# A reciprocal RMS spread by two fp32r products instead of fp32 ones, and four reorderings, in a hybrid S5 / RG-LRU decoder layer

## The chip, the core and the metric

One NeuronCore of a Trainium2 chip runs the whole layer. Its engines work side by side: TensorE (PE in the profile; PEld is its weight loading), VectorE (DVE), ScalarE (ACT), GpSimd (POOL) and SyncE (SP, which issues most DMAs). Each engine takes its instructions in the order in which the program wrote them; engines wait for each other by semaphores. The metric is device time in microseconds (us) of one execution, and the times given are medians over executions.

## What is computed

One layer, batch 1, 1024 tokens, model width 1024, all in float32:

```python
h = rms_norm(x, g_pre)
s5_x, s5_g, lru_x, lru_g, gate_s, gate_l = split(h @ w_in)      # w_in: 1024 x 5632
y_s = s5_ssm(s5_x, ...)                                         # 32 groups, 64 complex states each
glu_a, glu_b = split(gelu(y_s) @ w_glu)
z_s = (glu_a * sigmoid(glu_b) * silu(s5_g)) @ w_bs
y_l = rg_lru(causal_depthwise_conv(lru_x, conv_w, conv_b), ...) # 1280 channels
z_l = (y_l * silu(lru_g)) @ w_bl
merged = sigmoid(gate_s) * z_s + sigmoid(gate_l) * z_l
x = x + rms_norm(merged @ w_out, g_post)
x = x + (p @ w_ple) * sigmoid(x @ w_ple_gate)
```

`rms_norm(x, g)` is x * rsqrt(mean(x*x) + 1e-6) * g for each token.

## The kernel before

**Layout and products.** Everything is kept transposed: channels on the 128 partitions, tokens along the free axis in two halves of 512 (`HALF`). A matrix product of float32 quality is made of three products in the format fp32r (`three`, L314): each operand is split into a high part, rounded to fp32r, and a low part, the remainder; high x high, high x low and low x high are summed in PSUM. ScalarE makes a high part by a copy (L222, L311, L728, L1364), VectorE the low part by a subtraction (L234, L312, L733, L1371).

**Weights.** `weight_plan` (L37) lists all weight blocks as quads of four 128x128 blocks, in the order of use. `Weights` loads them in raw chunks through SP's queue (four raw buffers), splits them into a ring of six quads, and keeps some quads ahead of TensorE (`ahead`, L244). For w_bs, w_out and the first half of w_ple_gate (`BY_DMA`) the low part is not made by VectorE: ScalarE writes the negated weights into the low part's place after the high copy (L225), and a GpSimd DMA adds the raw weights onto it (L226). Some products for w_bl and w_out use sums of weight blocks, made by GpSimd (`sum`, L179, `add` at L194, marked by the quad "O2"): a quad's sums are issued only when all quads ahead of it have been split (L186).

**Order.** TensorE, VectorE, ScalarE and GpSimd run in the order written out by hand (`manual_schedule`, L480). Work beside the main products is put into generators, which `tick` (L328) advances by one step at each group of products.

**The start.** Eight fp32 warm-up products (L496), then p @ w_ple, column by column (m = 0..7, L755): each column is a PSUM tile `ps_ple` of two banks from a pool of three (`wide`). p comes in four quarters, two blocks of channels k by two halves of tokens; the order of loads is at L504, the first quarter on ScalarE's DMA queue, the rest on SP's. A dictionary `plan` (L747) says what follows each column: squares of x (`square`, L702) and their additions on VectorE (L713), splits of further weight quads (`weights`), and evictions of finished columns (`evict`, L741, by ScalarE to SBUF and by DMA to `ple_d`).

**The reciprocal RMS and its spread.** `tok_rstd` (L383) is a generator of three steps, used once ahead of the input projections ("pre", all 1024 tokens, eight chunks) and once for each token half of the output norm ("post1", then "post0", four chunks each). Step 1: products of the summed squares with a column of ones (`pst`, L388) put the sums of 128 tokens on the 128 partitions. Step 2: variance, square root on ScalarE (L393), reciprocal and one Newton step on VectorE (L394 to L398) give r; then, for each chunk, the identity matrix times r, a diagonal matrix (L401, VectorE). Step 3: an all-ones fp32 matrix times each diagonal matrix (L406) puts r of each token onto all 128 partitions, in the PSUM tile `psb`, one 128x128 product for each chunk. For "pre", steps 1 and 2 are issued after column 5 of w_ple and step 3 inside column 7. Then `h_hi` (L724) scales x by r (VectorE, L727) and splits it, and the first columns of w_in (`ps_u`) begin.

**The end.** merged @ w_out runs as a sequence of `product` calls (L1492) with operands T1 to T4, B11 to B22. `post_half(1)` (L1544) scales the second token half's mix by r and adds x, row by row (L1562, L1563), splitting each row for the last product. `gate_half(1)` (L1569) computes sigmoid(x @ w_ple_gate) for that half, `post_half(0)` advances meanwhile, then `gate_half(0)` follows. In `gate_half(1)` the first two output columns are computed side by side (L1575): the first four rows k of column 0, the same of column 1, then the last four of each. `finish` (L1588) applies the sigmoid on ScalarE, multiplies by p @ w_ple and adds x on VectorE. ScalarE's functions live in tables; changing between square root and sigmoid costs an ACT_TABLE_LOAD.

Of the kernel before, what the change touches and what calls it, by code (L numbers as in the profile page):

```python
# [17 lines left out]
P = 128  # L18
# [18 lines left out]
def weight_plan():  # L37
# [70 lines left out]
    for h in range(2):  # L108
        if not h:
            for ks in (lo, hi):  # L110
                cut(chunk(col("w_ple_gate", 0, ks) + col("w_ple_gate", 1, ks)))
        for c in cs[0 if h else 2:]:
            cut(c)
# [18 lines left out]

LAST = chunk_users()


class Weights:
# [42 lines left out]
    def sum(self, upto):  # L179
        G = self.nc.gpsimd  # L180
        while len(self.ready) <= min(upto, len(QUADS) - 1):
# [3 lines left out]
            s = self.sums  # L185
            if q[0] == "O2" and len(self.done) < i:  # L186
                return
# [25 lines left out]
    def make(self, upto):  # L213
        nc = self.nc
        while len(self.done) <= min(upto, len(QUADS) - 1):
            i = len(self.done)
            self.sum(i)
            src, n = self.ready[i]
            t = self.ring.tile([P, 2, 4, P], F32R, tag="q", name=f"wq{i}")
            hi = t[:, 0].rearrange("p b m -> p (b m)")[:, :n * P]  # L220
            lo = t[:, 1].rearrange("p b m -> p (b m)")[:, :n * P]
            nc.scalar.activation(hi, src, AF.Copy)  # L222
            q = QUADS[i]
            if q[0] == "plain" and BLOCKS[q[1][0]][0] in self.BY_DMA and i < len(QUADS) - 2 * ND:
                nc.scalar.activation(lo, src, AF.Copy, scale=-1.0)  # L225
                nc.gpsimd.dma_start(lo.bitcast(F32), src, accum_op=ALU.add)  # L226
            else:
                self.owed.append((i, lo, src, hi))
            self.done.append(t)
# [23 lines left out]
def tile_hybrid_trunk(  # L253
# [22 lines left out]
    def page(i, name, dt=F32R):  # L276
        return page_pool[i].tile([P, 2 * NT], dt, tag=f"pg{i}", name=name)
# [16 lines left out]
    ones = cst([P, P], "ones", 1.0)  # L294
    ident = cst([P, P], "ident")
    make_identity(nc, ident)
    halfpi = cst([P, 1], "halfpi", math.pi / 2)
    cp_t = cst([P, sum(n for _, n in CPAR)], "cp_t")
    sp8 = cst([P, NL], "sp8")
    nsp8 = cst([P, NL], "nsp8")  # L300
    cp = {}
    o = 0
# [80 lines left out]
    def tok_rstd(v, ssqs, n, name, res, diag):  # L383
# [5 lines left out]
        yield  # L389
        v = v.rearrange("p (i n) -> p i n", i=4)  # L390
        var, r, t, sd = (v[:, i, :nch] for i in range(4))
# [6 lines left out]
        V.tensor_tensor(r, r, t, ALU.mult)  # L398
        diag = diag.rearrange("p (c t) -> p c t", c=nch)
        for c in range(nch):  # L400
            V.tensor_scalar(diag[:, c, :], ident, r[:, c:c + 1], None, ALU.mult)  # L401
        yield
        for h in range(n // HT):
            pb = px.tile([P, HT], F32, tag="px", name=f"psb_{name}_{h}")
            for c in range(4):
                T.matmul(pb[:, c * P:(c + 1) * P], ones, diag[:, 4 * h + c, :], start=True, stop=True)  # L406
            res.append(pb)
# [68 lines left out]
    pt = scratch[:, :NPT]  # L476
    braw = page(7, "braw", F32)

# [16 lines left out]
    warm = px.tile([P, HT], F32, tag="px", name="warm")  # L495
    for _ in range(8):  # L496
        T.matmul(warm[:, :P], ones, ones, start=True, stop=True)
# [5 lines left out]
    W.fetch(0)  # L503
    for k in range(2):  # L504
        for h in range(2):
            (nc.sync if k or h else nc.scalar).dma_start(pf[:, k, HALF[h]], p[k * P:(k + 1) * P, HALF[h]])
    load_x(range(0, 3))
# [17 lines left out]
    V.tensor_tensor(p_lo[:, 0, HALF[0]], pf[:, 0, HALF[0]], p_hi[:, 0, HALF[0]].bitcast(F32), ALU.subtract)  # L525
    for k in range(2):
        for h in range(0 if k else 1, 2):
            split(p_hi[:, k, HALF[h]], p_lo[:, k, HALF[h]], pf[:, k, HALF[h]])
# [187 lines left out]
    ssqs = [ssq]  # L716
    stats = tok_rstd(pro.tile([P, 4 * ND], F32, name="rs_pre"), ssqs, NT, "pre", rb, sdp[:, 1])
    hq = {}
# [36 lines left out]
    for m in range(ND):  # L755
        if m % 2 == 0:
            wb = W.next()
        ps = wide(f"ps_ple{m}")
        rows_ps.append(ps)
        for k in range(2):  # L760
            for h in range(2):
                three(ps[:, HALF[h]], wb[2 * (m % 2) + k], (p_hi[:, k, HALF[h]], p_lo[:, k, HALF[h]]), k == 0, k == 1,
                      xl_last=m == 0)
            if k == 0 and m == 7:
                next(stats)
        if m == 5:
            next(stats)
            next(stats)
        for f, a in plan[m]:
            f(a)  # L770
            if f is square:
                add_squares(1)
        if m == 3:
            add_squares(0)
        W.fetch(9)
# [4 lines left out]
    evict(7)  # L780
    h_hi(1)
    nc.sync.dma_start(braw[:, :1024], spar[:, NPT:NPT + 1024])
    S.activation(d_skip, pt[:16, NPT - 32:], AF.Copy)
# [760 lines left out]
    def post_half(h):  # L1544
# [4 lines left out]
        add_square(h)  # L1549
        st = tok_rstd(dg[:, 2, 32 * h:32 * h + 32], [ssq[h]], HT, f"post{h}", out_, dg[:, h, :])  # L1550
        if h == 0:
# [17 lines left out]
    def gate_half(h, hl):  # L1569
# [4 lines left out]
        if h:  # L1574
            for n in range(4):  # L1575
                q, m = n // 2, n % 2
                if not q:
# [36 lines left out]

    dg = quarter(page(PG[1], "diags", F32))
    bg.append(post_half(1))
# [78 lines left out]
```

## Time and profile before

| | |
|---|---|
| time, median of 3 executions | 932.66 us (932.24 to 932.68) |
| the profiled execution: time / its span | 932.37 us / 930.6 us |
| mean granted TensorE clock | 0.999 |
| DMA over the span | 134.21 MB, mean 144 GB/s |

Busy time by stage, from windows of the trace (us; the windows end where the products of the stage do):

| window | work | PE | DVE | ACT | POOL |
|---|---|---|---|---|---|
| 0 to 38.6 | w_ple, norm, first of w_in | 36.59 | 28.14 | 24.74 | 6.04 |
| 38.6 to 308 | w_in gates, S5 branch | 269.36 | 169.67 | 106.16 | 64.08 |
| 308 to 580 | RG-LRU branch | 272.00 | 176.76 | 174.28 | 0.00 |
| 580 to 705 | w_bl, w_glu | 125.00 | 90.47 | 57.03 | 24.37 |
| 705 to 759 | w_bs, merge | 54.00 | 34.78 | 19.02 | 11.22 |
| 759 to 834.3 | w_out | 75.00 | 63.27 | 43.68 | 33.58 |
| 834.3 to 930.6 | w_ple_gate, output | 91.14 | 61.85 | 44.69 | 11.04 |

How to read the rows that follow. A row of the timeline has the start in the span and the duration, both in us, the engine, the line of the kernel, the operation, "written<-read" by tile names, the shape, and, in brackets, how long the engine had been idle and what released it; "x2" means two such instructions merged into one row. Products follow each other faster than one of them lasts: a 128x512 product lasts 0.39 us, and the next starts 0.23 us after it. A row of the waits has the waiting engine and line, the releaser, and the wait in total, its count and the longest.

### The profile page before, as it was taken

Reading aid. Unit: us, or ns where it says so; the run is one execution under the profiler, and the core shown is the slowest. Engines: PE = TensorE matmul, PEld = TensorE weight load, DVE = VectorE, ACT = ScalarE, POOL = GpSimd, SP = SyncE. Lnnn points to the kernel's source line nnn. Section 1 sums busy time; section 2 is a strip of 40 time slices with the busy share of each in tenths; the row PEclk is TensorE's granted clock in tenths of the full one; section 3 lists DMA queues with packets and bytes.
Section 4 is the critical chain, followed back from the end, with each engine's and each line's share of the span. In section 5 each row is a group of like instructions: output and inputs, shape, how many; then the busy total and the mean of one; then the engine's idle time right before and its main releaser. Section 6 shows DMA issues by size and latency. Waiting matters only on the chain.

```text
span 930.6 us, 11716 instructions
## 1 busy us (share of the span) xinstructions
PE 923.1 (99%) x4228; PEld 759.7 (82%) x4228; DVE 625.0 (67%) x977; ACT 469.6 (50%) x714; POOL 150.3 (16%) x159
## 2 busy tenths in 40 slices
PE   9999999999999999999999999999999999999997
PEld 7888888888888888888888888888888887887876
DVE  6985566666664446776666667687862798886863
ACT  6643233444443257666666668444434355558531
POOL 1318012212220000000000000022322126422100
PEclk9999999999999999999999999999999999999999
DMA  9745456554623211111111117811479965499951
GB/s 356 277 126 158 126 141 168 173 166 138 178 90 107 74 29 52 51 51 45 52 51 51 52 44 208 296 41 57 141 261 238 271 164 203 122 244 231 301 181 52
DMA packets 70442, 134.21 MB, mean 144 GB/s; under 512 B 18416, under 2 KB 32880, under 8 KB 70384
## 3 DMA queue, kind: packets, MB, share of 16 engines
q1 hardware_dynamic: 64768, 122.72, 41.5%
q0 software_dynamic: 5472, 10.49, 6.5%
q8 instruction: 33, 0.54, 0.2%
q10 hardware_dynamic: 144, 0.26, 0.1%
q14 instruction: 25, 0.20, 0.1%
HBM read 95.30 MB, written 27.53 MB: 132 GB/s over the span
## 4 chain that ended last, share of the span: by engine, by line
PE 96%; DVE 2%; issue 0%; DMA 0%; ACT 0%
PE ps_L L318 16%; PE ps_L L316 8%; PE ps_rg L318 8%; PE ps_rx L318 8%; PE ps_pg L318 6%; PE ps_rx L316 4%; PE ps_rg L316 4%; PE ps_F L318 3%; PE ps_u L318 3%; PE bZ L318 3%; PE ps_pg L316 3%; PE pg L318 2%; PE bW L318 2%; PE bX L318 2%; PE ps_ple L318 2%; PE ps_ea L318 2%
## 5 line engine op out<-in xcount | busy, mean ns | idle before, releaser
L318 PE MATMUL ps_L<-hB,wq 128*128 128x512 f32 x640 | 197.4, 390 | 0.0
L318 PEld LDWEIGHTS ps_L<-hB,wq 128*128 128x128 f32 x640 | 120.2, 188 | 24.5
L316 PE MATMUL ps_L<-hB,wq 128*128 128x512 f32 x320 | 127.0, 397 | 0.0
L222 ACT ACTIVATE wq<-wraw 128x512 fp32r<-128x512 f32 (+1 forms) x188 | 112.5, 614 | 24.3 <-issue 9.4
L234 DVE TENSOR_TENSOR wq<-wraw,wq 128x512 fp32r<-128x512 f32 (+1 forms) x152 | 104.0, 700 | 3.2 <-ACT wq L222 3.2
L318 PE MATMUL ps_rg<-hB,wq 128*128 128x512 f32 x320 | 98.7, 390 | 0.0
L318 PE MATMUL ps_rx<-hB,wq 128*128 128x512 f32 x320 | 98.7, 390 | 0.0
L318 PE MATMUL ps_pg<-x1hl,wq 128*128 128x512 f32 x240 | 75.2, 394 | 0.5 <-DVE x1hl L1371 0.5
L316 PEld LDWEIGHTS ps_L<-hB,wq 128*128 128x128 f32 x320 | 60.1, 188 | 13.4 <-issue 1.7
L318 PEld LDWEIGHTS ps_rg<-hB,wq 128*128 128x128 f32 x320 | 60.1, 188 | 12.9
L318 PEld LDWEIGHTS ps_rx<-hB,wq 128*128 128x128 f32 x320 | 60.1, 188 | 12.9
L1075 DVE SCALAR_TENSOR_TENSOR c<-ps_rx,cp_t,c 128x1023 f32<-128x1023 f32 (+2 forms) x30 | 38.5, 1282 | 47.6 <-ACT c L1073 46.9
L194 POOL TENSOR_TENSOR wS<-wraw 128x512 f32<-128x512 f32 x8 | 11.9, 1486 | 356.8 <-DMA wraw<-w_blocks 349.4
L316 PE MATMUL ps_rx<-hB,wq 128*128 128x512 f32 x160 | 62.5, 391 | 0.0
L316 PE MATMUL ps_rg<-hB,wq 128*128 128x512 f32 x160 | 62.5, 391 | 0.0
L318 PEld LDWEIGHTS ps_pg<-x1hl,wq 128*128 128x128 f32 x240 | 44.7, 188 | 11.8 <-DVE x1hl L1371 1.8
L1012 ACT ACTIVATE sg<-ps_L 128x1024 f32<-128x1024 f32 x20 | 20.5, 1026 | 59.6 <-issue 52.5
L226 POOL DMA_DIRECT2D wq<-wraw x36 | 31.8, 883 | 100.7 <-ACT wq L225 68.7
L316 PE MATMUL ps_pg<-x1hl,wq 128*128 128x512 f32 x120 | 47.1, 393 | 0.0
L318 PE MATMUL ps_u<-hB,wq 128*128 128x512 f32 x128 | 39.7, 392 | 0.4 <-DVE hB L733 0.4
L318 PE MATMUL ps_F<-ys,wq 128*128 128x512 f32 x128 | 39.4, 389 | 0.0
L1083 ACT ACT_TABLE_LOAD x9 | 11.5, 1283 | 51.2 <-DVE yr L1112 51.2
(360 smaller groups left out, 1930.4 us busy)
## 6 DMA issues: line engine op xcount, KB each, us to landing
wraw<-w_blocks SPq DMA_DIRECT2D x95, 512.0 KB
wq<-wraw POOLq DMA_DIRECT2D x36, 256.0 KB, 5.5
xt<-x_t SPq DMA_DIRECT2D x8, 512.0 KB
ple_d<-ple_sb SPq DMA_DIRECT2D x8, 512.0 KB
wn<-sbt SPq DMA_DIRECT2D x8, 512.0 KB
sgl_d<-sg SPq DMA_DIRECT2D x8, 512.0 KB
wn<-pt_d SPq DMA_DIRECT2D x16, 256.0 KB
sgs_d<-sg SPq DMA_DIRECT2D x8, 512.0 KB
```

Of the source, the lines that this page charges most:

```text
L194: G.tensor_tensor(s[name], s[a], s[b], op)
L222: nc.scalar.activation(hi, src, AF.Copy)
L226: nc.gpsimd.dma_start(lo.bitcast(F32), src, accum_op=ALU.add)
L234: self.nc.vector.tensor_tensor(lo, src, hi.bitcast(F32), ALU.subtract)
L316: T.matmul(ps, wh, xh, start=start, stop=False, skip_group_check=more)
L318: T.matmul(ps, a, b, start=False, stop=stop and a is (wh if xl_last else wl), skip_group_check=more)
L1012: S.activation(t, ps, AF.Sigmoid)
L1075: V.scalar_tensor_tensor(c[:, d:], ps[:, :NT - d], w_[3 - d], c[:, d:], ALU.mult, ALU.add)
L1083: S.activation(sq, ps, AF.Sigmoid)
```

## The change

Five things, in one diff:

1. `tok_rstd`'s spread: r is split into a high part `rh` (fp32r) and a remainder `rl`. VectorE makes the diagonal matrices of the high part, ScalarE those of the remainder (a copy of the identity scaled by a column of `rl`), and the spread is two fp32r products of 128x512 for each token half, with a matrix of ones in fp32r, in place of four fp32 products of 128x128. The diagonal matrices lie in other pages ("pre": page 7, so the page's later use `braw` is opened later; "post": all of `dg`), and the small columns of "post" in a tile of their own.
2. `gate_half(1)` computes the first three columns of w_ple_gate side by side in place of two, and the weight plan has the third column's quads between the others.
3. The sums of the first w_out quad with sums may be issued one quad earlier; the quad ahead of it has its low part made by VectorE in place of the GpSimd DMA.
4. p is loaded by token halves, all four quarters in SP's queue, and split in that order.
5. Columns 0 and 1 of p @ w_ple are computed together, product by product, by token half; seven warm-up products in place of eight.

```diff
@@ weight_plan @@
-            for ks in (lo, hi):
+            for i, ks in enumerate((lo, hi)):
                 cut(chunk(col("w_ple_gate", 0, ks) + col("w_ple_gate", 1, ks)))
-        for c in cs[0 if h else 2:]:
+                quads.append(("plain", cs[2], 4 * i, 4))
+        for c in cs[0 if h else 3:]:
             cut(c)
@@ Weights @@
+FIRST_OUT = max(i for i, q in enumerate(QUADS) if q[0] == "O2") - 12
+BY_V = (FIRST_OUT - 1,)
+AHEAD = {i: i == FIRST_OUT for i, q in enumerate(QUADS) if q[0] == "O2"}
-            if q[0] == "O2" and len(self.done) < i:
+            if q[0] == "O2" and len(self.done) < i - AHEAD[i]:
                 return
-            if q[0] == "plain" and BLOCKS[q[1][0]][0] in self.BY_DMA and i < len(QUADS) - 2 * ND:
+            if q[0] == "plain" and BLOCKS[q[1][0]][0] in self.BY_DMA and i < len(QUADS) - 2 * ND and i not in BY_V:
                 nc.scalar.activation(lo, src, AF.Copy, scale=-1.0)
                 nc.gpsimd.dma_start(lo.bitcast(F32), src, accum_op=ALU.add)
@@ constants @@
+    ones_r = cst([P, P], "ones_r", dt=F32R)
+    V.tensor_copy(ones_r, ones)
+    rhl = cst([P, ND], "rhl", dt=F32R)
+    rs_post = cst([P, 40], "rs_post")
@@ tok_rstd @@
-        v = v.rearrange("p (i n) -> p i n", i=4)
+        v = v.rearrange("p (i n) -> p i n", i=5)
...
-        diag = diag.rearrange("p (c t) -> p c t", c=nch)
+        dh, dl = (t_.rearrange("p (c t) -> p c t", c=nch) for t_ in diag)
+        rh, rl = rhl[:, :nch], v[:, 4, :nch]
+        V.tensor_copy(rh, r)
+        V.tensor_tensor(rl, r, rh.bitcast(F32), ALU.subtract)
         for c in range(nch):
-            V.tensor_scalar(diag[:, c, :], ident, r[:, c:c + 1], None, ALU.mult)
+            V.tensor_scalar(dh[:, c, :], ident, r[:, c:c + 1], None, ALU.mult)
+            S.activation(dl[:, c, :], ident, AF.Copy, scale=rl[:, c:c + 1])
         yield
         for h in range(n // HT):
             pb = px.tile([P, HT], F32, tag="px", name=f"psb_{name}_{h}")
-            for c in range(4):
-                T.matmul(pb[:, c * P:(c + 1) * P], ones, diag[:, 4 * h + c, :], start=True, stop=True)
+            for d, e in zip(diag, (True, False)):
+                T.matmul(pb, ones_r, d[:, h * HT:(h + 1) * HT], start=e, stop=not e)
@@ start @@
-    for _ in range(8):
+    for _ in range(7):
         T.matmul(warm[:, :P], ones, ones, start=True, stop=True)
-    for k in range(2):
-        for h in range(2):
-            (nc.sync if k or h else nc.scalar).dma_start(pf[:, k, HALF[h]], p[k * P:(k + 1) * P, HALF[h]])
+    for h in range(2):
+        for k in range(2):
+            nc.sync.dma_start(pf[:, k, HALF[h]], p[k * P:(k + 1) * P, HALF[h]])
...
-    for k in range(2):
-        for h in range(0 if k else 1, 2):
+    for h in range(2):
+        for k in range(0 if h else 1, 2):
             split(p_hi[:, k, HALF[h]], p_lo[:, k, HALF[h]], pf[:, k, HALF[h]])
@@ p @ w_ple, in the loop over m @@
-        ps = wide(f"ps_ple{m}")
-        rows_ps.append(ps)
+        if m != 1:
+            rows_ps.append(wide(f"ps_ple{m}"))
+        if m == 0:
+            rows_ps.append(wide("ps_ple1"))
+            for h in range(2):
+                for k in range(2):
+                    for i, j in ((0, 0), (1, 0), (0, 1)):
+                        for t in range(2):
+                            T.matmul(rows_ps[t][:, HALF[h]], wb[2 * t + k][i], (p_hi, p_lo)[j][:, k, HALF[h]],
+                                     start=k == i == j == 0, stop=k == j == 1)
+        ps = rows_ps[m]
         for k in range(2):
-            for h in range(2):
-                three(..., xl_last=m == 0)
+            for h in range(2 if m > 1 else 0):
+                three(...)
@@ post_half, gate_half @@
-        st = tok_rstd(dg[:, 2, 32 * h:32 * h + 32], [ssq[h]], HT, f"post{h}", out_, dg[:, h, :])
+        st = tok_rstd(rs_post[:, 20 * h:20 * h + 20], [ssq[h]], HT, f"post{h}", out_, (dg[:, 2 * h, :], dg[:, 2 * h + 1, :]))
-            for n in range(4):
-                q, m = n // 2, n % 2
+            for n in range(6):
+                q, m = n // 3, n % 3
```

## What was predicted, and from which rows

> **What bounds the kernel now.** The page is read first, then TensorE's waits, then each engine's timeline around those waits.
>
> ```profile
> PE 923.1 (99%) x4228; PEld 759.7 (82%) x4228; DVE 625.0 (67%) x977; ACT 469.6 (50%) x714; POOL 150.3 (16%) x159
> PE 96%; DVE 2%; issue 0%; DMA 0%; ACT 0%
> PE ps_ple L316 <- ACT wq L222: 0.6, 1, 0.6
> PE ps_pg L318 <- DVE x1hl L1371: 0.5, 1, 0.5
> PE ps_u L318 <- DVE hB L733: 0.4, 1, 0.4
> PE oY L318 <- DVE wq L234: 0.3, 1, 0.3
> ```
>
> TensorE (PE) is busy for 99% of the span and 96% of the chain that ended last. Its waits are all in three places: the first 42 us, one spot at 772 us, and the stretch after 840 us. Between 39 and 771 us it waits for nothing, so a shift made at the start is carried through whole. The change touches exactly these places, and what matters there is which wait ends last.
>
> **Start (p by halves, two w_ple columns together, one warm-up product fewer, one small copy more): 0.**
>
> ```profile
> 7.73 0.63 PE L318 MATMUL ps_ple<-p_hi,wq 128*128 128x512 f32 x1
> 11.93 0.63 ACT L222 ACTIVATE wq<-wraw 128x512 fp32r<-128x512 f32 x1 [2.18 <-DMA wraw<-w_blocks]
> 13.21 5.38 DVE L713 TENSOR_TENSOR sdp<-sdp,sqs 128x1024 f32<-128x1024 f32 x3
> 16.29 0.63 ACT L222 ACTIVATE wq<-wraw 128x512 fp32r<-128x512 f32 x1 [0.83 <-DMA wraw<-w_blocks]
> 19.11 5.21 DVE L713 TENSOR_TENSOR sdp<-sdp,sqs 128x1024 f32<-128x1024 f32 x4
> 24.37 1.95 PE L388 MATMUL pst_pre<-ones,sdp 128*128 128x1 f32 x16
> ```
>
> The pairing lets TensorE run without its early gaps (0.6 us and less). But the statistics product at 24.37 needs the last addition of squares, which ends at 19.11 + 5.21 = 24.32. That chain on VectorE (DVE) has no slack: DMA delivers the second weight block at 11.93, its remainder precedes the first addition, and from 13.21 the seven additions fill 5.38 + 5.21 us with one more remainder between. The order of x and of that weight block in the queue does not change. What TensorE gains earlier it waits off at 24.37. The eviction of column 0 moves to the end of the paired columns, near 13, yet ScalarE (ACT) waits for a DMA until 16.29 anyway. Where that cover is gone, the half microsecond of delay would reach the additions. Bounds: -0.1 and +0.2 (one queue instead of two at first; no row shows either, and I take them from the 0.05 between 24.32 and 24.37 and from half of the 0.40 that one issue takes).
>
> **Spread before the u columns: +3.1.** It replaces 8 fp32 products (16 records) by 4 fp32r products, and adds two small VectorE operations and eight ScalarE copies scaled by a column.
>
> ```profile
> 26.55 0.21 ACT L393 ACTIVATE rs_pre<-rs_pre 128x8 f32<-128x8 f32 x1 [3.53 <-DVE rs_pre L392]
> 26.67 1.01 ACT L743 ACTIVATE ple_sb<-ps_ple 128x1024 f32<-128x1024 f32 x1
> 27.57 0.62 ACT L222 ACTIVATE wq<-wraw 128x512 fp32r<-128x512 f32 x1
> 29.00 1.15 ACT L222 ACTIVATE wq<-wraw 128x512 fp32r<-128x512 f32 x2
> 27.64 0.17 DVE L398 TENSOR_TENSOR rs_pre<-rs_pre 128x8 f32<-128x8 f32 x1
> 29.41 1.89 DVE L234 TENSOR_TENSOR wq<-wraw,wq 128x512 fp32r<-128x512 f32 x3
> 31.49 1.64 DVE L727 SCALAR_TENSOR_TENSOR xt<-xt,cp_t,psb_pre 128x512 f32<-128x512 f32 x2 [0.18 <-PE psb_pre L406]
> 29.03 0.39 PE L316 MATMUL ps_ple<-p_hi,wq 128*128 128x512 f32 x1
> 30.39 1.95 PE L406 MATMUL psb_pre<-sdp,ones 128*128 128x128 f32 x16
> 32.10 0.48 PE L316 MATMUL ps_ple<-p_hi,wq 128*128 128x512 f32 x1
> L1609 ACT ACTIVATE sbp<-ps_pgz 128x128 f32<-128x128 f32 x2 | 0.4, 274 | 2.4 <-PE ps_pgz L318 2.4
> ```
>
> On TensorE the old spread costs 32.10 - 30.39 = 1.71; the six products between 29.03 and 30.39 give 0.227 each, so the new one costs 4 x 0.227 = 0.91: 0.80 less. That is not what ends last. ScalarE works in program order: the eviction of column 4 (26.67) had its data long before, yet came only behind the square root. The eight scaled copies now stand between these two. They need the remainder of r: r is there at 27.81, two more operations at 0.2 each (0.17 busy and the hand-over) make 28.2.
>
> Price of one scaled copy: no row shows it. The nearest is the 128x128 activation, 274 ns; overlapped it could be 0.18, with the added pointer 0.37. I take 0.27, so 8 x 0.27 = 2.16 and ScalarE is free at 30.4 instead of 26.67: 3.7 later. The Trainium skill ("ScalarE: Activation LUTs", What ACT_TABLE_LOAD costs) prices an ACTIVATE at 186 ns + 0.833 ns per element, 93 ns more for a pointer operand and 93 less back to back, an estimate of 0.29 here; the sum by it is 0.2 higher in this place.
>
> What waits: column 7 (first product 29.03) takes the PSUM buffer of column 4, whose eviction now ends at 31.4. TensorE idles 2.4, and the spread inside column 7 comes at 32.8. Worse, behind that eviction stand the three weight copies; the last ended at 30.15 and now ends at 33.88. VectorE's remainder of it (0.69, the last of the three from 29.41) precedes the first scaling of x in program order, which starts at 34.6 instead of 31.49: **+3.1**. TensorE follows that scaling (its ps_u wait above), so the 0.80 is lost. Bounds: 8 x 0.18 gives +2.4, 8 x 0.37 gives +3.9.
>
> **w_out sums sooner: -0.45 there, 0 at the end.**
>
> ```profile
> 768.93 0.64 ACT L222 ACTIVATE wq<-wS 128x512 fp32r<-128x512 f32 x1 [2.69 <-POOL wS L194]
> 771.75 0.39 PE L318 MATMUL oY<-mT,wq 128*128 128x512 f32 x1
> 772.43 0.50 PE L318 MATMUL oY<-mT,wq 128*128 128x512 f32 x1 [0.30 <-DVE wq L234]
> ```
>
> ScalarE waited 2.69 for GpSimd's sums and with it the remainder TensorE needed. One product (12 x 0.227 = 2.7) sooner removes it: 772.43 - 771.75 - 0.23 = 0.45. Of the quad before, the remainder moves from a GpSimd DMA, which would stand behind the sums, to VectorE; that is one operation of 0.69 on an engine busy 67%. Bounds -0.45 and 0 (raw weights late).
>
> **Spread of the second half and the three columns: no gain at 857.**
>
> ```profile
> 821.21 0.92 DVE L401 TENSOR_SCALAR diags<-ident,diags 128x128 f32<-128x128 f32 x4
> 822.44 1.05 PE L406 MATMUL psb_post<-diags,ones 128*128 128x128 f32 x8
> 841.33 0.63 ACT L1364 ACTIVATE x1hl<-x 128x512 fp32r<-128x512 f32 x1 [1.35 <-DVE x L1563]
> 841.95 0.73 PE L318 MATMUL ps_pg<-x1hl,wq 128*128 128x512 f32 x2 [0.47 <-DVE x1hl L1371]
> 846.26 0.90 PE L318 MATMUL ps_pg<-x1hl,wq 128*128 128x512 f32 x2
> 848.23 1.28 ACT L1589 ACT_TABLE_LOAD   x1
> 857.24 0.95 PE L388 MATMUL pst_post<-ones,ssq 128*128 128x1 f32 x8
> ```
>
> Here the spread is 2 x 0.227 instead of 0.81, but the copies end at 821.21 + 0.4 + 4 x 0.27 = 822.7, so the last product ends 0.3 sooner than before and VectorE starts so much earlier; with the 0.45 that makes 0.8. The three columns remove the stall at 841.95 (0.6 and two of 0.1). Two things are late next. The remainder of the fifth weight group, made by ScalarE only behind the last x1hl copy (841.33) and then by a DMA, already stalls TensorE at 846.26; reached 0.8 sooner, it keeps it just as long. And the statistics at 857.24 now wait: six groups of three ScalarE operations (1.15 - 0.62 = 0.53 apart, from the pair at 29.00) instead of four precede the table load, from 841.9 - 0.8 to 850.6; load and first sigmoid (1.28, 0.60) end at 852.5; VectorE's six finishing operations and the last addition, 7 at about 0.67, end at 857.1. So the statistics move -0.14.
>
> **Spread of the first half: +2.55, with the -0.14 +2.4.**
>
> ```profile
> 858.42 0.21 ACT L393 ACTIVATE diags<-diags 128x4 f32<-128x4 f32 x1 [0.32 <-DVE diags L392]
> 858.64 1.28 ACT L1589 ACT_TABLE_LOAD   x1
> 859.67 0.88 DVE L401 TENSOR_SCALAR diags<-ident,diags 128x128 f32<-128x128 f32 x4
> 859.94 0.60 ACT L1589 ACTIVATE sbp<-ps_pg 128x512 f32<-128x512 f32 x1
> 860.57 0.69 DVE L1590 TENSOR_TENSOR sbp<-sbp,plp 128x512 f32<-128x512 f32 x1
> 884.63 1.48 DVE L1371 TENSOR_TENSOR x1hl<-x,x1hl 128x512 fp32r<-128x512 f32 x2
> 886.18 0.70 PE L318 MATMUL ps_pg<-x1hl,wq 128*128 128x512 f32 x2
> ```
>
> Four copies follow the square root, from 859.67 + 0.4 = 860.1 (remainder of r) to 861.2; only then come the table load (1.30 to the next operation) and the sigmoid (0.60), so VectorE's finish of column 3 starts at 863.1 instead of 860.57, and the rows of x behind it shift alike, down to the last x1hl at 886.1, for which TensorE already waits at 886.18. That chain is serial, VectorE and ScalarE by turns. Bounds: copies at 0.18 and 0.37, and the statistics up to 0.7 sooner: +1.7 to +2.8.
>
> **Sum**, on the profiled execution's 932.37: + 0 + 3.1 + 2.4 = **937.9** (the median of the three runs, 932.66, is 0.29 above it, so the basis is no matter). Own range, from both places' bounds: 932.37 + 2.4 + 1.7 = 936.5 to 932.37 + 4.1 + 2.8 = 939.3.
>
> **Rivals.** *One hold only* (15%): idle time of VectorE's last chain absorbs the first-half delay, leaving 935.5, or weight copies are not behind the eviction, leaving 934.8; I say 935.2. Against: the old rows show both orders. *The other side, faster* (11%): the shorter products end last. Place: ScalarE at 26.67; price: 0.80 + 2 x 0.36 + 0.45 + 0.84 = 2.8, so 929.6. It decides if column 4's eviction ends before 29.03, that is if the copies are through by 28.0; for it speaks only that ScalarE idles 3.53 ahead of the square root. *The clock* (8%): the product at 7.73 takes 0.63, that at 29.03 takes 0.39, so TensorE starts slow; if the longer gap ahead of the first product, or the idle 2.4, holds it slow for ten more of them, ten times some 0.2 less what the next wait hides, about 1 us, is added: 939. The Trainium skill ("TensorE: Matmul & The Clock Gate", Part 1) has the gate watch windows of about 3.4 us, which the idle 2.4 would not fill. *Nothing measurable* (5%): the copies overlap wholly, 932.4. My forecast has 61%.
>
> A measurement of this kernel tells about 0.2%, 1.9 us, from no change. Faster 0.11 is the second rival; same 0.07 is the last and the low end of one hold; slower 0.82. The range leaves out the faster rival and a tail of the clock: 933.0 to 939.8.
>
> **What would show it.** Eight ScalarE copies ahead of column 4's eviction; a TensorE gap of about 2.4 before column 7 with that eviction as releaser; the first scaling of x near 34.6; no wait at 772; the first-half sigmoid behind copies and table load, and a TensorE wait of some 3 us in the first column of the last half. I am wrong if that eviction still starts near 27, or if the last x1hl comes no later against the statistics than 28.9 us (886.1 - 857.2).

## The result, and the profile after

The changed kernel takes **940.92 us** (median of four executions, 939.61 to 940.99) against 932.67 before (four executions, 932.24 to 932.71): a ratio of 1.0087, 95% interval 1.0075 to 1.0100. It is 8.25 us slower. Forecast were 937.9 and a range up to 939.8: the sign was right, the size too small. The profiled execution is the shortest of the four: 939.61 us, a span of 937.8 against 930.6.

From the page of the changed kernel, the busy times and the shares of the chain that ended last:

```profile
PE 923.1 (98%) x4202; PEld 757.3 (81%) x4202; DVE 627.6 (67%) x985; ACT 473.5 (50%) x729; POOL 149.5 (16%) x158
PE 86%; DVE 5%; issue 3%; DMA 2%; ACT 2%; SPq 0%; POOL 0%; DVEq 0%; POOLq 0%; ACTq 0%
```

TensorE's work is 923.1 us as before, to a tenth. All that came on top is waiting, and its share of the chain fell from 96% to 86%. Where it waits, three lines from the list of waits of the changed kernel (total, count, longest):

```profile
PE ps_pg L326 <- DMA wq<-wraw: 2.9, 3, 1.6
PE ps_ple L324 <- ACT ple_sb L755: 2.5, 1, 2.5
PE oX L326 <- DVE wq L238: 0.9, 1, 0.9
```

None of the three was on the list before; that of 0.3 in oY is gone. Rows of the changed kernel's timeline, in order of place:

```profile
12.26 0.63 ACT L226 ACTIVATE wq<-wraw 128x512 fp32r<-128x512 f32 x1 [2.15 <-DMA wraw<-w_blocks]
24.69 1.95 PE L396 MATMUL pst_pre<-ones,sdp 128*128 128x1 f32 x16
26.87 0.21 ACT L401 ACTIVATE rs_pre<-rs_pre 128x8 f32<-128x8 f32 x1 [3.54 <-DVE rs_pre L400]
28.57 2.44 ACT L413 ACTIVATE spread<-ident,rs_pre 128x128 fp32r<-128x128 f32 x8 [1.49 <-DVE rs_pre L410]
30.91 1.00 ACT L755 ACTIVATE ple_sb<-ps_ple 128x1024 f32<-128x1024 f32 x1
31.97 0.50 PE L324 MATMUL ps_ple<-p_hi,wq 128*128 128x512 f32 x1 [2.46 <-ACT ple_sb L755]
33.90 1.29 DVE L238 TENSOR_TENSOR wq<-wraw,wq 128x512 fp32r<-128x512 f32 x2 [0.74 <-ACT wq L226]
35.11 1.40 DVE L739 SCALAR_TENSOR_TENSOR xt<-xt,cp_t,psb_pre 128x512 f32<-128x512 f32 x2
...
773.22 0.50 PE L326 MATMUL oX<-mB,wq 128*128 128x512 f32 x1 [0.93 <-DVE wq L238]
822.28 0.95 PE L396 MATMUL pst_post<-ones,ssq 128*128 128x1 f32 x8
850.12 0.50 PE L326 MATMUL ps_pg<-x1hl,wq 128*128 128x512 f32 x1 [0.79 <-DMA wq<-wraw]
859.11 0.50 PE L326 MATMUL ps_pg<-x1hl,wq 128*128 128x512 f32 x1 [0.48 <-DMA wq<-wraw]
861.54 1.02 PE L396 MATMUL pst_post<-ones,ssq 128*128 128x1 f32 x8
864.44 1.28 ACT L413 ACTIVATE diags<-ident,rs_post 128x128 fp32r<-128x128 f32 x4 [1.44 <-DVE rs_post L410]
865.74 1.28 ACT L1610 ACT_TABLE_LOAD   x1
867.03 0.60 ACT L1610 ACTIVATE sbp<-ps_pg 128x512 f32<-128x512 f32 x1
867.66 0.69 DVE L1611 TENSOR_TENSOR sbp<-sbp,plp 128x512 f32<-128x512 f32 x1 [2.47 <-ACT sbp L1610]
869.00 0.68 DVE L1583 TENSOR_TENSOR mix<-mix,psb_post 128x512 f32<-128x512 f32 x1
876.49 0.50 PE L326 MATMUL ps_pg<-x1hl,wq 128*128 128x512 f32 x1 [1.59 <-DMA wq<-wraw]
892.40 0.73 PE L326 MATMUL ps_pg<-x1hl,wq 128*128 128x512 f32 x2 [0.83 <-DVE x1hl L1392]
```

In the kernel before, the row that answers to the one at 869.00, where VectorE begins with the first half's rows of x:

```profile
861.96 0.69 DVE L1562 TENSOR_TENSOR mix<-mix,psb_post 128x512 f32<-128x512 f32 x1
```

The two holds are there as the prediction drew them: eight copies between square root and eviction, TensorE waiting 2.46 for that eviction, the first scaling of x at 35.11 instead of 31.49; then four copies ahead of the table load, the sigmoid and VectorE's finish. The wait of some 3 us in the first column of the last half came in two pieces: 1.59 for a remainder by DMA and 0.83 for the last x1hl.

Every kernel of this study runs the same work between a few landmarks, so four distances place each loss. **A**: from the first statistics product (`pst_pre`) to the first scaling of x. **B**: from the first product of oX to the statistics product of the second half. **C**: from there to that of the first half. **D**: from there to the first row of x (VectorE's first operation that reads `psb_post`). All are differences of starts in the timelines (oX begins at 755.19 before and at 758.08 after, the statistics of the second half stand at 818.77 and 822.28); "start" is where `pst_pre` stands.

| kernel | median us | start | A | B | C | D |
|---|---|---|---|---|---|---|
| before | 932.67 | 24.37 | 7.12 | 63.58 | 38.47 | 4.72 |
| after | 940.92 | 24.69 | 10.42 | 64.20 | 39.26 | 7.46 |

In the profiled execution the start is 0.32 later, A 3.30 longer, B 0.62, C 0.79 and D 2.74; from the first scaling to oX 0.73 come back (723.70 before, 722.97 after). What brings the 0.73 back was not traced. The sum is 7.04, the 869.00 - 861.96 by which the first row of x is late, and nearly all of the 7.2 by which the span is longer.

### The profile page after: what moved, and what is told of

Its sections match the earlier page's. It is cut to its first block, busy times and chain, and to the rows that moved or that the text cites. A ratio compares the mean times of both kernels' runs of the same rounds, so it can differ in the third digit from the quotient of the medians.

```text
span 937.8 us, 11683 instructions
## 1 busy us (share of the span) xinstructions
PE 923.1 (98%) x4202; PEld 757.3 (81%) x4202; DVE 627.6 (67%) x985; ACT 473.5 (50%) x729; POOL 149.5 (16%) x158
## 4 chain that ended last, share of the span: by engine, by line
PE 86%; DVE 5%; issue 3%; DMA 2%; ACT 2%; SPq 0%; POOL 0%; DVEq 0%; POOLq 0%; ACTq 0%
PE ps_L L326 16%; PE ps_L L324 8%; PE ps_rx L326 8%; PE ps_rg L326 8%; PE ps_rg L324 4%; PE ps_rx L324 4%; PE ps_u L326 3%; PE bZ L326 3%; PE ps_pg L326 3%; PE ps_F L326 3%; PE pg L326 2%; PE bW L326 2%; PE bX L326 2%; PE ps_ea L326 2%; PE ps_eb L326 2%
```

## The experiments

**Theory**: the spread costs by ScalarE's program order, in two places (A and D); the start costs by its one DMA queue, the earlier sums cost B, the three columns C. **Rivals**: one hold only counts; the reorderings are harmless or only bite together; the extra 1.3 us of the longer executions is the clock.

| kernel | median us | ratio to before, 95% interval | start | A | B | C | D |
|---|---|---|---|---|---|---|---|
| e1 old spread | 935.23 | 1.0028 (1.0016 to 1.0039) | 26.72 | 7.02 | 64.21 | 39.68 | 4.71 |
| e2 spread alone | 938.46 | 1.0060 (1.0048 to 1.0073) | 24.82 | 10.42 | 63.59 | 38.40 | 7.39 |
| e3 start alone | 933.53 | 1.0008 (1.0000 to 1.0017) | 25.91 | 7.11 | 63.56 | 38.44 | 4.72 |
| e4 eviction first | 939.58 | 1.0076 (1.0062 to 1.0090) | 25.27 | 9.00 | 64.84 | 39.38 | 7.38 |
| e5 sums alone | 933.23 | 1.0008 (1.0000 to 1.0017) | 24.50 | 6.97 | 64.20 | 38.47 | 4.72 |
| e6 columns alone | 933.68 | 1.0009 (1.0001 to 1.0018) | 24.21 | 7.09 | 63.68 | 39.84 | 4.72 |
| e9 start, two queues | 932.38 | 0.9998 (0.9989 to 1.0007) | 24.25 | 7.10 | 63.52 | 38.44 | 4.72 |
| e10 before, one queue | 933.54 | 1.0011 (1.0002 to 1.0020) | 24.98 | 7.10 | 63.55 | 38.45 | 4.72 |
| e11 first spread alone | 936.04 | 1.0037 (1.0024 to 1.0050) | 24.96 | 10.96 | 64.03 | 38.49 | 4.72 |
| e12 no ScalarE copies | 935.05 | 1.0029 (1.0018 to 1.0041) | 24.17 | 8.69 | 66.69 | 38.64 | 5.61 |
| e14 columns, low parts by VectorE | 931.38 | 0.9989 (0.9980 to 0.9998) | 24.42 | 7.10 | 63.55 | 37.29 | 4.71 |
| e13 two parts | 931.38 | 0.9987 (0.9978 to 0.9995) | 24.32 | 7.11 | 63.81 | 37.29 | 4.71 |
| e15 changed again | 941.66 | 1.0104 (1.0087 to 1.0121) | 25.43 | 11.00 | 64.25 | 39.25 | 7.46 |
| e16 changed, two queues | 939.62 | 1.0084 (1.0069 to 1.0099) | 24.47 | 10.42 | 64.79 | 39.26 | 7.46 |

In the main each part moves its own distance. B has a second, passing cause: in e11 and e12 TensorE waits 0.5 and 1.8 in oX for a remainder by DMA, in e4 and e16 1.56 and 1.5 for the one that the earlier sums delay, where the changed kernel waits 0.93. The trace of e12 is of its slowest execution (937.07). The start varies by itself: in the ten traces with two queues it lies between 24.17 and 24.96, so the 0.32 of the first trace shows nothing alone. Alone, the parts cost 5.77 (spread, against 932.69), 0.84 (start, against 932.69), 0.58 (sums) and 1.03 (columns, both against 932.65): 8.22, and the whole change costs 8.25. That the two agree so closely is luck: the interval of the spread's ratio alone is over 2 us wide, and the changed kernel run again (e15) costs 9.33, against 932.33. The intervals of the small parts are as wide as the parts. For the sums and the columns it is the distances that make them sure; for the start it is the medians of eleven executions each (e3 and e10 against e9).

### The spread

e1 and e2, the whole spread taken out of the change, and put alone into the kernel before. The heart of e1's edit, shortened; e2's is the reverse:

```diff
-            S.activation(dl[:, c, :], ident, AF.Copy, scale=rl[:, c:c + 1])
...
-            for d, e in zip(diag, (True, False)):
-                T.matmul(pb, ones_r, d[:, h * HT:(h + 1) * HT], start=e, stop=not e)
+            for c in range(4):
+                T.matmul(pb[:, c * P:(c + 1) * P], ones, diag[:, 4 * h + c, :], start=True, stop=True)
```

> The changed kernel with the old fp32 spread put back at all three places; the other four parts stay. Theory: the spread's ScalarE copies are most of the loss (3.05 us ahead of the u columns, 2.7 us in the first token half, both read from the trace of the changed kernel), the rest is 0.3 at the start and about 0.7 between w_out and the statistics of the first half. So the time falls from 940.9 to between 933.2 and 934.2, and the first scaling of x comes back to about 31.8. Rival: the reorderings (three columns, sums sooner, one queue for p) are the loss and the spread only shows where it falls; then the time stays above 938.

> The kernel before with the new spread alone. Theory: its two holds add up whatever stands around them: 932.65 + 3.05 + 2.7 = 938.4, between 937.8 and 939.0. Rival: the holds only bite together with the three columns (six groups of ScalarE work ahead of the table load); then the second one is under 1 us and the time is under 936.7. Third: the extra 1.3 us of three of the four executions of the changed kernel belongs to the spread (the idle time at column 7); then 939.7.

e2 came as expected: 938.46. e1 takes A and D back to 7.02 and 4.71, so both belong to the spread, but its 935.23 lies a microsecond above what was expected: the start (26.72) and C (39.68) are worse than one trace of the changed kernel had shown. Those two are taken up below.

e4, ScalarE's order at the first place (shortened; the two operations leave their old place behind column 5):

```diff
         if m == 5:
             next(stats)
+            evict(4)
+            weights(4)
             next(stats)
```

> The changed kernel with the eviction of column 4 and the weight copies of the fifth quad put ahead of the statistics' second step, so ahead of the eight scaled copies on ScalarE. Theory: column 7 no longer waits 2.46 us for its PSUM buffer, and ScalarE has one eviction (1.0) and one copy (0.63) less behind the scaled copies; the last of VectorE's remainders and with it the first scaling of x comes 1.6 earlier, near 33.5: 939.3. Rival: the hold is not ScalarE's order but the longer chain from the statistics to the spread itself; then the first scaling stays near 35.1 and the time at 940.9.

939.58, A 1.42 shorter. ScalarE had been free for it: the eviction and the copy fit into the 3.5 us in which it used to wait for the square root's input. The rest of A stands, since one eviction, two weight copies and two remainders still follow the scaled copies.

e11, the new spread at the first place only, and e12, no scaled copies on ScalarE, both from e2 and shortened:

```diff
 e11, in tok_rstd; for four chunks the old code follows
+        if nch == 4:
+            diag = diag.rearrange("p (c t) -> p c t", c=nch)
...
 e12, in effect
-            S.activation(dl[:, c, :], ident, AF.Copy, scale=rl[:, c:c + 1])
+        for c in range(nch):
+            V.tensor_scalar(dl[:, c, :], ident, rl[:, c:c + 1], None, ALU.mult)
```

> The kernel before with the new spread ahead of the input projections alone; the two later spreads stay fp32. Theory: the two holds of the spread are separate places on one serial course, so this one alone costs its 3.05 whole: 932.65 + 3.05 = 935.7, between 935.3 and 936.1, and the chain of the first half stands as before (first row of x 4.72 after the statistics). Rival, one hold only: later slack takes back part of it, under 934.7.

> The kernel before with the new spread alone (938.46), but the diagonal matrices of the remainder are made by VectorE behind those of the high part, none by ScalarE. Theory: the hold is ScalarE's program order. Without the copies there, the eviction of column 4 follows the square root at once (26.9 instead of 31.0), the sigmoid of the first half too; what is left is VectorE's longer chain. By its 0.21 a piece the first scaling of x starts near 33.7 instead of 35.2, the first row of x in the first half 1.6 sooner: 935.4. Rival: the chain through the remainder is as long on either engine; then 938.4.

e11: 936.04, 3.60 above the 932.44 of its kernel before, so nothing later takes the first hold back, and "one hold only" falls. e12: 935.05, better than expected. Its timeline:

```profile
26.34 0.21 ACT L397 ACTIVATE rs_pre<-rs_pre 128x8 f32<-128x8 f32 x1 [3.53 <-DVE rs_pre L396]
26.46 1.01 ACT L755 ACTIVATE ple_sb<-ps_ple 128x1024 f32<-128x1024 f32 x1
29.49 1.66 DVE L413 TENSOR_SCALAR spread<-ident,rs_pre 128x128 fp32r<-128x128 f32 x8
31.05 1.90 DVE L234 TENSOR_TENSOR wq<-wraw,wq 128x512 fp32r<-128x512 f32 x3
32.86 1.41 DVE L739 SCALAR_TENSOR_TENSOR xt<-xt,cp_t,psb_pre 128x512 f32<-128x512 f32 x2
```

The eviction follows the square root at once, as before the change. What is left of A, 8.69 against 7.12, is about the 1.56 from the start of the remainder's matrices (29.49) to the start of the next operation (31.05), on VectorE. So taking the copies off ScalarE gives back 1.73 of the 3.30. What remains here is VectorE's own eight operations; it is not a second half of the changed kernel's loss, where VectorE makes no matrices of the remainder and waits for ScalarE's weight copies (0.74 at 33.90). Either way the products that are shorter on TensorE do not pay for eight more operations ahead of them.

### The start

e3 is the kernel before with parts 4 and 5 of the diff alone; e9 and e10 change one queue:

```diff
 e9, in e3
-            nc.sync.dma_start(pf[:, k, HALF[h]], ...)
+            (nc.sync if k or h else nc.scalar).dma_start(pf[:, k, HALF[h]], ...)
 e10, in the kernel before
-            (nc.sync if k or h else nc.scalar).dma_start(pf[:, k, HALF[h]], ...)
+            nc.sync.dma_start(pf[:, k, HALF[h]], ...)
```

> The kernel before with the start alone: p by token halves in one queue, columns 0 and 1 of p @ w_ple together, seven warm-up products. Theory: VectorE's additions end 0.3 later as in the changed kernel, because the transfers land 0.33 later, and nothing takes it back: 932.65 + 0.3 = 932.95. Rival: the clock; the shorter warm-up leaves TensorE slow for a stretch more in most executions, and this is the extra 1.3 us: 934.2. Third: nothing, 932.65.

> The start alone as before (933.53 against 932.69), but with the first quarter of p on ScalarE's DMA queue again; the order by token halves, the pairing and the seven warm-up products stay. Theory: it is the one queue that costs; from 4 to 6 us the transfers are back at some 360 GB/s (180 to 290 in the kernels with one queue), the first square of x starts at 8.7 and the weight copy ahead of the additions near 12.0: 932.7, between 932.3 and 932.9. Rival: the order by halves costs; the rate from 4 to 6 us stays under 300 and the time at 933.5.

> The kernel before with the first quarter of p moved from ScalarE's to SP's queue, nothing else. Theory: the one queue is what costs, so the loss of the start appears whole: 933.5 (933.0 to 934.2, wider spread between executions than before), the rate from 4 to 6 us under 300 GB/s. Rival: the order by halves or the pairing costs: 932.7, rate some 360.

e3 came out between theory and rival, 0.84 slower, and its trace shows full clock but the statistics product at 25.91. e9 and e10 decide: the move to one queue alone, without pairing or order, costs 0.89 (933.54), and the start with two queues costs nothing (932.38). The window from 4 to 6 us of the kernel before (the last two numbers are the DMA engines' busy share and GB/s):

```profile
4.00:6.00 2.00, 1.39 (x5) 0.83 (x4) 1.06 (x3) 1.20 (x2) 0.00 (x0) 1.00 1.03 361
```

The same window of e10, with one queue:

```profile
4.00:6.00 2.00, 1.94 (x6) 1.12 (x5) 1.63 (x3) 0.22 (x1) 0.00 (x0) 1.00 0.93 257
```

And of e9, with two:

```profile
4.00:6.00 2.00, 0.96 (x4) 0.42 (x3) 1.09 (x3) 1.23 (x2) 0.00 (x0) 1.00 1.00 362
```

With one queue the rate in this window is 257 GB/s, in the other traces with one queue 181 (e4) to 292 (the changed kernel), and in the ten with two 334 to 379, while the engines count as mostly busy. Two things changed with the queue, and no run separates them. SP issues a fourth load of p ahead of x, so the first load of x is issued at 3.07 (e10) instead of 2.60; and the rate falls. The second weight block's copy starts 0.62 later in e10 (12.55 for 11.93), which the 0.47 of issue could mostly cover, but 1.07 later in e15 and 1.54 in e3, which it could not. Why the rate falls was not tried. The Trainium skill ("DMA: Bandwidth & Descriptors", Issuing engines are not separate DMA queues) says that a second issuing engine saves only the time to issue. Here that time is the 0.47, the second queue is worth 0.89 us in the median, and the measurement decides.

### The sums of w_out

e5 is the kernel before with part 3 of the diff alone:

```diff
-            if q[0] == "O2" and len(self.done) < i:
+            if q[0] == "O2" and len(self.done) < i - AHEAD[i]:
...
+ and i not in BY_V
```

> The kernel before with the w_out sums one block sooner alone (and the low part of the quad ahead by VectorE). Theory from the trace of the changed kernel: GpSimd's three sums now lie on three VectorE operations (0.69 us becomes 1.8 to 2.2 each) that stand ahead of the remainder of the quad before; TensorE waits some 0.9 in oX for that remainder and no longer 0.3 in oY. The stretch from the first oX product to the statistics of the second half, 63.58 before, becomes 64.2: 932.7 + 0.6 = 933.3. Rival, the prediction's own step: the wait in oY goes and nothing comes, 932.2 or, if a later wait takes the gain, 932.7.

933.23, B 64.20. The timeline of e5:

```profile
761.69 2.17 DVE L1391 TENSOR_TENSOR mtmp<-mg,mg 128x512 f32<-128x512 f32 x1
761.70 1.61 POOL L197 TENSOR_TENSOR wS<-wraw 128x512 f32<-128x512 f32 x1
763.39 1.64 POOL L197 TENSOR_TENSOR wS<-wS,wraw 128x512 f32<-128x512 f32 x1
763.79 1.78 DVE L1393 TENSOR_TENSOR mg<-mg,mg 128x512 f32<-128x512 f32 x1
764.98 1.74 POOL L197 TENSOR_TENSOR wraw<-wraw,wraw 128x512 f32<-128x512 f32 x1
765.49 1.78 DVE L1374 TENSOR_TENSOR mT<-mtmp,mT 128x512 fp32r<-128x512 f32 x1
769.61 0.68 DVE L237 TENSOR_TENSOR wq<-wraw,wq 128x512 fp32r<-128x512 f32 x1
770.34 0.50 PE L321 MATMUL oX<-mB,wq 128*128 128x512 f32 x1 [0.93 <-DVE wq L237]
```

VectorE's operations of this shape take 0.69 by themselves. Beside a sum on GpSimd they take 1.78 to 2.17, so the three lose about 3.7 us together (2.17 + 1.78 + 1.78 - 3 x 0.69). The remainder that was moved to VectorE stands behind them, and TensorE waits 0.93 for it in oX. The old wait of 0.3 went, a larger one came in the quad before. The price could have been read before the change, where the same sums ran from 765.57 to 770.60 and slowed two of VectorE's operations:

```profile
765.75 3.70 DVE L1371 TENSOR_TENSOR mT<-mg,mT 128x512 fp32r<-128x512 f32 x2 [0.75 <-ACT mT L1364]
```

The earlier sums and the moved remainder were not run apart, so how much each of the two costs stays open.

### The three columns

e6 is the kernel before with part 2 of the diff alone (six groups instead of four, and the plan to match); e14 adds one exception in the weights, so that the low parts of six quads are VectorE's; e13 is e14 with the start of e9.

```diff
+BY_V = range(len(QUADS) - 28, len(QUADS) - 22)
...
-            if q[0] == "plain" and BLOCKS[q[1][0]][0] in self.BY_DMA and i < len(QUADS) - 2 * ND:
+            if q[0] == "plain" and BLOCKS[q[1][0]][0] in self.BY_DMA and i < len(QUADS) - 2 * ND and i not in BY_V:
```

> The kernel before with three columns side by side alone. Theory: TensorE trades the short waits for x1hl at 842 for waits for the remainders that come by DMA (about 0.9 near 846 and 0.5 to 0.9 near 855), so the statistics of the first half stand 39.3 to 39.7 after those of the second, not 38.47, and the end moves alike: 933.5 to 933.9. Rival, the prediction's step: the two late things cancel the gain, the distance stays within 0.2 of 38.47 and the time at 932.5 to 932.9.

> The kernel before with three columns side by side alone (933.68), and the low parts of the fifth to tenth quads of w_ple_gate made by VectorE, not by ScalarE's second copy and GpSimd's DMA. Theory: what TensorE waits for at 846.6 and 856.1 is the remainder by DMA, and the six groups of three ScalarE operations (1.56 us a group) are what sets the pace behind the last x1hl copy; with two operations a group the table load comes 3 us sooner, VectorE has room between the additions (it idles 0.87 in each group), both waits go, and the distance of the two statistics falls from 39.84 to 38.0 or less: 931.8 to 932.3. Rival: VectorE's order puts the remainders behind other work, and waits of some size for VectorE come instead: 933.0 to 933.8.

> The parts that may be worth keeping together: the paired start with the first quarter of p on ScalarE's DMA queue, and three columns with the six low parts by VectorE; no new spread, no earlier sums. Theory: their moves add, -0.3 from the start (932.38 against 932.65) and what the columns give: 931.5 to 932.1. Rival: the start's gain is within the spread between executions and the columns give nothing: 932.5 to 932.9.

The timeline of e6, one group of ScalarE's operations and TensorE's waits:

```profile
843.35 0.62 ACT L223 ACTIVATE wq<-wraw 128x512 fp32r<-128x512 f32 x1
843.87 0.62 ACT L226 ACTIVATE wq<-wraw 128x512 fp32r<-128x512 f32 x1
844.39 0.62 ACT L1485 ACTIVATE sq<-mix 128x512 f32<-128x512 f32 x1
846.59 0.50 PE L319 MATMUL ps_pg<-x1hl,wq 128*128 128x512 f32 x1 [0.88 <-DMA wq<-wraw]
856.13 0.50 PE L319 MATMUL ps_pg<-x1hl,wq 128*128 128x512 f32 x1 [0.99 <-DMA wq<-wraw]
```

The timeline of e14, one group:

```profile
842.92 0.62 ACT L224 ACTIVATE wq<-wraw 128x512 fp32r<-128x512 f32 x1
843.45 0.62 ACT L1486 ACTIVATE sq<-mix 128x512 f32<-128x512 f32 x1
```

In e6 the stall of 0.47 for x1hl is gone as meant, and TensorE waits 0.88 and 0.99 instead, both times for a remainder that comes by DMA. C grows by 1.37, the time by 1.03. In e14 a group on ScalarE has two operations, not three, VectorE makes the remainders in gaps that it had, both waits are gone, and C is 37.29: 1.18 shorter than before the change. At 931.38 us (ratio 0.9989, 0.9980 to 0.9998) e14 is **the version that beats both kernels**, by 0.1% and about 1 us. The three columns cost time with their weights late and not with their weights on time. VectorE's low parts with two columns were not run, so what the columns themselves give in e14 is not shown. Before the change both had something to remove: the stall of 0.47 for x1hl, and one of about 0.28 for a remainder by DMA at 846.26 (0.90 for two products that elsewhere take 0.62). e13 came out a little better than expected, but the paired start adds nothing to e14.

### The longer executions

Three of the changed kernel's four executions took 1.3 us more than the profiled one, at a mean granted clock of 0.996 to 0.998 instead of 1.000. e15 is the changed kernel with nothing edited; e16 has the edit of e9.

> The changed kernel again, nothing edited, for the trace of an execution near 940.9 (three of four were). Theory A, transfers: the statistics product of the start stands at 25.5 or later (24.69 in the first trace) and the distances behind it are as in the first trace (10.42, 39.26, 7.46). Theory B, clock: it stands near 24.7, the granted clock between 27 and 42 us is under 0.95, the products behind TensorE's idle time are 0.43 apart, and the first scaling of x or the first oX product comes 1 us or more later than in the first trace.

> The changed kernel with the first quarter of p on ScalarE's DMA queue again, all else as changed. Theory A: the transfers of the start are the 1.3 us and the 0.32 of the first trace: 939.2 to 939.7, with the statistics product near 24.3. Theory B, the clock after the idle time: only 0.3 to 0.8 goes, 940.1 to 940.6.

The profiled execution of e15 took 941.07, with a span of 939.3. Its timeline at TensorE's idle time:

```profile
25.43 1.95 PE L396 MATMUL pst_pre<-ones,sdp 128*128 128x1 f32 x16
29.82 0.39 PE L326 MATMUL ps_ple<-p_hi,wq 128*128 128x512 f32 x1
32.72 0.69 PE L324 MATMUL ps_ple<-p_hi,wq 128*128 128x512 f32 x1 [2.50 <-ACT ple_sb L755]
33.20 0.63 PE L326 MATMUL ps_ple<-p_lo,wq 128*128 128x512 f32 x1
33.63 0.63 PE L326 MATMUL ps_ple<-p_hi,wq 128*128 128x512 f32 x1
```

Its window from 27 to 42 us (the third number from the end is the granted clock):

```profile
27.00:42.00 15.00, 12.29 (x48) 9.40 (x48) 10.41 (x28) 10.76 (x23) 0.56 (x1) 0.89 0.51 193
```

Both theories hold, each for a part. The start is 0.74 later than in the first trace (25.43 - 24.69), and behind the idle 2.50 the products follow each other 0.43 apart instead of 0.23, so that the spread inside column 7 is late and A is 0.58 longer. Together that is 1.32, of a span that is 1.5 longer. e16 lies where theory A put it, at 939.62, with the start at 24.47. It is 2.04 below e15, more than the queue cost in the kernel before; with four executions each that difference is not sure. Its trace shows a clock of 0.89 in the same window too, but there the products slowed later, and A stayed at 10.42; its longer B (64.79) is the wait of 1.5 in oX. Of six traces with 2 us or more of idle time between 27 and 42 us, five have 0.89 in that window (e2, e4, e11, e15, e16), and only the first trace of the changed kernel has 1.00. The same shows elsewhere: behind a wait of 2.04 at 13.84 in e1 and of 1.82 at 771.88 in e12 the products are 0.43 apart as well, and this adds to e12's long B. A wait of 1.83 in e4 (at 877.62) and all those of 0.9 to 1.7 us after the first 12 us have no such stretch. What it costs depends on where it sets in: A is 10.96 and 11.00 where the first product behind the idle time is slow already (e11, e15), 10.42 where the fourth is (e2, e16).

## Why the prediction was right or wrong

- **Spread before the u columns, +3.1**: right in mechanism and place; eviction, TensorE's gap (2.46 for 2.4) and first scaling stand where it put them. A grew by 3.30. A scaled copy takes 0.31 (2.44 / 8), not 0.27. The Trainium skill's 0.29 ("ScalarE: Activation LUTs", What ACT_TABLE_LOAD costs) was the nearer estimate. But "TensorE follows that scaling, so the 0.80 is lost" is not what was measured: 0.73 came back by oX, though no run shows that it is the same 0.80.
- **Spread of the first half, +2.55**: right, D grew by 2.74; four copies took 1.28 where 1.08 was counted.
- **Start, 0, bounds -0.1 and +0.2**: wrong. That TensorE's gain would be waited off at the statistics was right (e9: 932.38). The step that failed is the price of one queue behind "the order of x and of that weight block in the queue does not change": the order stayed, but x was issued 0.47 later and the rate fell. One queue was bounded by half of one issue's time, 0.2; the start was 0.32 later in the first trace, 1.06 in e15, and the queue costs 0.89 in the median of e10.
- **w_out sums sooner, -0.45 there, 0 at the end**: the old wait went, as said. What failed is the price of the moved remainder, "one operation of 0.69 on an engine busy 67%". 67% is the share of the whole run; at that place VectorE had a queue that GpSimd's own sums made longer. B grew by 0.62, outside the bounds.
- **Second half and three columns, -0.14**: wrong, C grew by 0.79. The chain of six groups, table load and finish was well priced: 16.6 from the last x1hl copy to the statistics (841.33 - 0.8 = 840.5 to 857.1), and it took 16.77 (844.77 to 861.54). What failed is the 0.8 by which that copy was to come sooner. 0.45 of it was the sums' gain, which did not come, and of the other 0.3 only 0.07 did (the copy stands 22.49 behind the statistics of the second half, 22.56 before). And that the fifth remainder would keep TensorE "just as long" missed that the eighth comes late too (0.48 here, 0.99 in e6). In the changed kernel the two limits nearly tie: in e15 TensorE waits 0.47 at the statistics for VectorE's last addition, in the first trace it does not.
- **The rivals**: "one hold only" fell with e11, "the other side" with every trace. "The clock" is the one that came, after the idle 2.4 as it said, but together with the forecast and not in its place; e15 puts 0.58 on it. The prediction cited a rule by which that gap would be too short (the Trainium skill, "TensorE: Matmul & The Clock Gate", Part 1, idle windows of about 3.4 us); e15 lost the clock after 2.50 and e12 after 1.82.
- **The sum**: 0 + 3.1 + 2.4 became 0.32 + 3.30 - 0.73 + 0.62 + 0.79 + 2.74 in the first trace. Both large terms were good to 0.2. The three that were set to nothing, start, sums and columns, are 1.73 of it, as much as lies between 937.9 and the profiled 939.61, which is still inside the range. The median leaves the range by the further 1.3 of the longer executions: in e15 0.74 of later start, again the queue's term or its own variation, and 0.58 of slow clock, which the forecast left out.

## What to carry to other kernels

Price an added operation by what stands behind it on its engine at that place, and put whatever is ready already ahead of it: the shorter products here were never what ended last. An engine that is busy 67% in the mean can be full where it matters, so a step is "covered" only by rows of the very microseconds into which it moves. And where a reordering takes away one wait, look for the data that is late next: the three columns lost 1 us with their weights as they were, and with the low parts made by another engine the kernel gained 1 us.

## What the runs showed of the hardware

- The four loads of p on one queue against one of them on a second: 257 against 361 GB/s from 4 to 6 us (e10, before); 181 to 292 in the six traces with one queue, 334 to 379 in the ten with two.
- VectorE's 128x512 operation of two SBUF operands takes 0.69, and 1.78 to 2.17 beside a GpSimd sum (e5); two of them took 3.70 beside one before the change.
- TensorE's products can be 0.43 apart instead of 0.23 after 2.50 (e15) and even 1.82 us (e12) of idle time, for some eight products of 128x512. Seven of the nine idle times of 1.8 us or more in these traces have it, two do not (2.46 in the first trace, 1.83 in e4).
